# A decoder layer in split fp32: a weight sum made one product earlier, other orders for two kinds of sets, the opening and the closing norm

## The chip, the cores and the metric

The kernel runs on one core of a Trainium2 chip. The metric is the device time of one launch in microseconds. One execution was also profiled; its trace gives the rows that are shown.

## The reference

The layer takes one prompt of 512 tokens, with 16 learned tokens ahead of it, and 8 single sample tokens, in fp32. It layer-normalises the input (2048 wide), projects it to queries, keys, values and a pooling input, runs windowed attention with sinks and a causal pooling mixer, projects both back, and ends with a SwiGLU block between two norms:

```python
h1 = layer_norm(DEEPNORM_ALPHA * h + mix, ln1_g, ln1_b)
a = jax.nn.silu(h1 @ w_gate) * (h1 @ w_up)        # w_gate, w_up: 2048 x 5632
ff = a @ w_down                                   # 5632 x 2048
return layer_norm(DEEPNORM_ALPHA * h1 + ff, ln2_g, ln2_b)
```

(Two lines are shortened here: the reference writes the products as einsum.) What is computed is the same in both kernels.

## The kernel before

**Number format.** TensorE works on operands that are split into a rounded high part and the rest. `split` (L181) makes them from a weight tile: a copy on ScalarE (ACT) for the high half (L185), a subtraction on VectorE (DVE) for the low half (L186). `products` (L198) then issues three matmuls where one would stand: high by high (L201), high by low (L202), low by high (L204).

**Products.** The large matrix products are made in 2 x 2 blocks with seven block products instead of eight (P1 to P7, Winograd's form). For that some operands are sums of weight blocks. `weight_sum` (L191) makes such a sum in place, on DVE (L194), over 128 x 1024 elements. A `Set` (L949) is one tile of 2 x 128 output features of w_gate (g) or w_up (u): four raw weight blocks (r, c), asked for by `q` from the DMA queue of SyncE (SP, L178), and seven products in `run` (L999). `prod` (L966) says which block or sum each takes: P1 takes (0,0), P2 (0,1), P4 (1,1); P7 takes S3 = (0,0) - (1,0), made in the place of (1,0); P6 takes (1,1) - (1,0), again in (1,0); P5 adds (1,0) to (0,0), in (0,0); P3 takes (0,1) - (1,0), in (0,1). Each product is split in two halves (`for g in range(2)`), each of 12 matmuls of 128 x 260.

**Rings.** Raw blocks come from a ring of NRAW = 5 tiles of 512 KB, split halves from a ring of WB = 5. A tile is written again when the tile five places before it in the ring has had its last reader, so the order in which the blocks are asked for decides what a load waits for.

**Sets.** There are 22 pairs (g, u), so 44 sets, and three kinds. In the first pair P1 and P2 are made ahead and stay in PSUM banks (`bk`, NKEEP = 2, "kept"). In the up sets of the next ten pairs P1 is made ahead and copied to SBUF (`p1`, NFILL = 10, "filled"). All others make their P1 themselves. `ahead` (L983) makes these products, before the first set, in plain fp32 (L988). After each product DVE or ACT combines the results: L1010 copies P1, L1022 or L1024 writes c22, L1028 or L1031 c21, L1036 c11, L1041 adds P5's bank to c22, L1045 adds to c21, L1050 writes c12. `al`, `ga`, `de` are PSUM banks; P5 and P3 write `al` after P6, so P3 has to wait until L1041 has read it.

**What sets the order.** On each engine instructions run in the order in which they were placed, one after the other. In most of the kernel a planner places them, by data dependences, its own cost estimates and priorities; loads, splits and weight sums get a priority that lets them go ahead of their place in the code (WPRIO = 400). In the opening the order on TensorE, DVE and ACT is written out by hand: `step` (L158) ties each group of instructions behind the group before.

**Opening (L418 to L480).** For each half h of the tokens the loop over g makes two steps of the key/value projection: `x_norm` (L349, its activation L339) normalises a 512-wide piece of x on ACT (and DVE for the extra rows), `x_turn` (L355, transposes L364) transposes it on TensorE, `x_split` (L366) scales and splits it (L370, L373, L376, L377), `kv_weights` splits weights, `kv_mm` multiplies. `stats` (L304) is a generator for the layer-norm statistics of one row block (L308, L311); those of the second half of x are in `later`, in two parts per block. `normalisers(1)` (L330) makes the factors from them.

**After the sets** the down projection (`column_pair`, L1190) runs in the same form, and the four tile rows that are left (PLAIN) follow as plain blocks: `down(h, m)` (L1295) for two halves of the columns h and 16 row blocks m, 12 matmuls each, added to `acc` by L1308. The closing norm is `Rows` (L1313): `part(q)` transposes a quarter of 128 tokens (L1322) into a bank, takes statistics from it (L1324), copies it to SBUF (L1325); `end` makes mean and deviation and applies them (L1332, L1333), a DMA for each quarter. Tokens of `rows[:2]` are ready after h = 0, those of `rows[2:]` after h = 1.

Of the kernel before, what the change touches and what calls it, by code (L numbers as in the profile page):

```python
# [1 line left out]

# [64 lines left out]
def hybrid_step(ctx, tc, xin, w_in, w_o, w_g, w_u, w_d, w_pool, par_d, cst_d, ident_d, ln2gb, kct_d, vc_d, hist_d,  # L67
                ck_d, cv_d, sp_d, yp, ys, nkp, nvp, npp, nks, nvs, nps):
    nc = tc.nc
# [183 lines left out]
    with ExitStack() as sa:  # L253
# [185 lines left out]
        for h in range(2):  # L439
            for g in range(4):  # L440
                n = h * 4 + g + 1
                with step(*three):
                    x_split(h, 2 * g + 1)
                    if n < 8 and n != 4:
                        x_norm(n // 4, n % 4)
                with step(*three):
                    kv_mm(h, 2 * g)
                if n < 8:
                    with step(*three):
                        x_turn(n // 4, n % 4)  # L450
                        if n < 7:
                            load_kvw((n + 1) % 4)
                        kvw.pop(n % 4, None)
                        kv_weights(n % 4, range(3))
                if h == 0 and g < 2:
                    with step(*three):
                        next(later.pop(0))
                if n < 8:
                    with step(*three):
                        x_split(n // 4, 2 * (n % 4))  # L460
                if n == 2:
                    with step(*three):
                        for x in later:
                            next(x)
                if n == 3:
                    with step(*three):
                        norm[1] = normalisers(1)
                        x_norm(1, 0)
                with step(*three):
                    kv_mm(h, 2 * g + 1)  # L470
                    if n < 8:
                        kv_weights(n % 4, [3])
            with step(*three):
                for i in range(4):
                    if i % 2:
                        nc.vector.tensor_scalar(zkv[i][:, XH[h]], out[i], par[:, PBIAS + i:PBIAS + i + 1], None,
                                                op0=ALU.add)
                    else:
                        nc.scalar.activation(zkv[i][:, XH[h]], out[i], AF.Identity, bias=par[:, PBIAS + i:PBIAS + i + 1])
                if h == 0:  # L480
                    out = kv_banks(1)
# [335 lines left out]
    def bank(name, w=HN):  # L817
        return ps.tile([P, 512], F32, tag="bank", name=name, bufs=banks)[:, :w]
# [130 lines left out]
    class Set:  # L949


        def __init__(self, w, i, name):
            self.w, self.i, self.name = w, i, name
            self.raw, self.bk, self.p1 = {}, {}, None

        def q(self, r, c):
            if (r, c) not in self.raw:
# [4 lines left out]
        def s(self, t, a, b, op):  # L962
            weight_sum(op, self.q(*t), self.q(*a), self.q(*b))
            return self.q(*t)

        def prod(self, n, bk, first=True):  # L966


            b = {1: "b11", 2: "b21", 3: "b22", 4: "t4", 5: "t1", 6: "t2", 7: "t3"}[n]
            src = {1: lambda: self.q(0, 0), 2: lambda: self.q(0, 1), 4: lambda: self.q(1, 1),  # L970
                   7: lambda: self.s((1, 0), (0, 0), (1, 0), nc.vector.tensor_sub),
                   6: lambda: self.s((1, 0), (1, 1), (1, 0), nc.vector.tensor_sub),
                   5: lambda: self.s((0, 0), (1, 0), (0, 0), nc.vector.tensor_add),
                   3: lambda: self.s((0, 1), (0, 1), (1, 0), nc.vector.tensor_sub)}[n]()
            for g in range(2):
                wh, wl = split(src[:, g * 512:(g + 1) * 512], f"{self.name}_{n}{g}")
                for kk in range(4):
                    k = 4 * g + kk
                    sl = slice(kk * P, (kk + 1) * P)
                    hi, lo = bop[b][k // 2]  # L980
                    products([bk], wh[:, sl], wl[:, sl], [hi[:, k % 2, :]], [lo[:, k % 2, :]], k == 0 and first, k == 7, True)
# [17 lines left out]
        def run(self, c11, c12, c21, c22, side=(), out=None):  # L999

            side = iter(side)
            r = row_tile(f"p_{self.name}")
            filled = self.p1 is not None
            al, de = [self.bk.get(n) for n in (1, 2)]
            if not filled:
                self.p1 = r[:, HALF[0]]
                if al is None:
                    al = bank(f"p1_{self.name}")
                    self.prod(1, al)
                nc.scalar.copy(self.p1, al)  # L1010
            else:
                al = bank(f"p1_{self.name}")
            ga = bank(f"p7_{self.name}")
            next(side, None)
            if filled and de is None:

                de = bank(f"p2_{self.name}")
                self.prod(2, de)
            self.prod(7, ga)
            next(side, None)  # L1020
            if filled:
                nc.vector.tensor_add(c22, ga, self.p1)  # L1022
            else:
                nc.scalar.copy(c22, ga)  # L1024
            self.prod(6, al, filled)
            next(side, None)
            if filled:
                nc.vector.tensor_add(c21, al, self.p1)  # L1028
                self.prod(4, ga, False)
            else:  # L1030
                nc.scalar.copy(c21, al)  # L1031
                if de is None:
                    de = bank(f"p2_{self.name}")
                    self.prod(2, de)
            next(side, None)
            nc.vector.tensor_add(c11, de, self.p1)  # L1036
            if out:
                out(0)
            self.prod(5, al, False)
            next(side, None)  # L1040
            nc.vector.tensor_add(c22, c22, al)  # L1041
            if not filled:
                self.prod(4, ga, False)
            next(side, None)
            nc.vector.tensor_add(c21, c21, ga)  # L1045
            if out:
                out(1)
            self.prod(3, al, False)
            if filled:
                nc.vector.tensor_add(c12, al, self.p1)  # L1050
                return c12
            return al
# [61 lines left out]
        bop[n] = [(slot(f"{n}h{i}"), slot(f"{n}l{i}")) for i in range(4)]  # L1114
    turn = [i for i in range(NPAIR) if i not in PLAIN] + [*PLAIN]
    sets = [Set(w, i, f"{n}{i}") for i in turn for n, w in (("g", w_g), ("u", w_u))]
    g1 = ln1(1, zs1)
    fills = [s.ahead(n) for n in (1, 2) for s in sets[:NKEEP]]
    for j, s in enumerate(sets[NKEEP + 1::2][:NFILL]):
# [193 lines left out]
    class Rows:  # L1313
# [4 lines left out]
        def part(self, q):  # L1318
            n, c0 = self.n, self.c0
            tp = bank(f"tz{c0}_{q}", 512)  # L1320
            for i in range(4):
                nc.tensor.transpose(tp[:n, i * P:(i + 1) * P], acc[4 * q + i][:, c0:c0 + n], ident)  # L1322
            z = zp.tile([P, 512], F32, tag="z", name=f"z{c0}_{q}", bufs=NZ)[:n]
            nc.vector.bn_stats(self.st[:n, q, :], tp[:n])  # L1324
            nc.scalar.copy(z, tp[:n])  # L1325
            self.z.append(z)

        def end(self):
            n = self.n
            mu, r = stats_end(pb, self.st, self.mv, n, f"z{self.c0}")  # L1330
            for q, z in enumerate(self.z):
                nc.vector.scalar_tensor_tensor(z, z, mu, gb[0][q][:n], op0=ALU.subtract, op1=ALU.mult)  # L1332
                nc.vector.scalar_tensor_tensor(z, z, r, gb[1][q][:n], op0=ALU.mult, op1=ALU.add)  # L1333
                nc.sync.dma_start(self.dst[:, q * 512:(q + 1) * 512], z)

    def sample_rows():

# [48 lines left out]
    for h, part in ((0, rows[:2]), (1, rows[2:])):  # L1386
        for m in range(KT):
            down(h, m)
            if h == 0 and m in (1, 2):
                for i, q in gb_loads[4 * m - 4:4 * m]:  # L1390
                    nc.sync.dma_start(gb[i][q], ln2gb[i:i + 1, q * 512:(q + 1) * 512].to_broadcast([P, 512]))
            if m % 4 == 3:
                for x in part:
                    x.part(m // 4)
            if (h, m) in ((0, 4), (0, KT - 1), (1, 4), (1, 10), (1, KT - 1)):
                next(sample)
        for x in part:
            x.end()


# [88 lines left out]
```

## Time and profile before

| | us |
|---|---|
| median of 3 runs | 1951.48 (1947.17 to 1955.55) |
| profiled execution | 1948.36 |
| its span, first to last instruction | 1946.5 |
| TensorE busy | 1900.8 (98%) |
| DVE busy | 1542.5 (79%) |
| ACT busy | 935.0 (48%) |
| mean granted TensorE clock | 0.995 |

The stages in the span: opening 0 to 80, attention and pooling to about 340, output projection and the products made ahead to about 590, gate/up sets to about 1450, down projection to about 1850, remainder and closing norm to the end. A row of a timeline gives start, length, engine, line of the kernel, operation, output and input by their names, and in brackets how long the engine was idle before and what ended that. A row that ends in x4 is four instructions in a run. A row of the waits gives engine, its tile and line, what it waited for, then the total, the number of times and the longest one.

### The profile page before, as it was taken

Reading aid. Unit: us, or ns where it says so; the run is one execution under the profiler, and the core shown is the slowest. Engines: PE = TensorE matmul, PEld = TensorE weight load, DVE = VectorE, ACT = ScalarE, POOL = GpSimd, SP = SyncE. Lnnn points to the kernel's source line nnn. Section 1 sums busy time; section 2 is a strip of 40 time slices with the busy share of each in tenths; the row PEclk is TensorE's granted clock in tenths of the full one; section 3 lists DMA queues with packets and bytes.
Section 4 is the critical chain, followed back from the end, with each engine's and each line's share of the span. In section 5 each row is a group of like instructions: output and inputs, shape, how many; then the busy total and the mean of one; then the engine's idle time right before and its main releaser. Section 6 shows DMA issues by size and latency. Waiting matters only on the chain.

```text
span 1946.5 us, 39267 instructions
## 1 busy us (share of the span) xinstructions
PE 1900.8 (98%) x15533; PEld 1865.5 (96%) x15533; DVE 1542.5 (79%) x2734; ACT 935.0 (48%) x1808; POOL 2.7 (0%) x9
## 2 busy tenths in 40 slices
PE   8999999999999999999999999999999999999996
PEld 8999999999989999999999999999999999999996
DVE  6666658768677888888888888888877888888877
ACT  5644445545554444454445555455554443444441
POOL 0000000000000000000000000000000000000000
PEclk9999999999999999999999999999999999999998
DMA  8722222666754444445444534445459564655332
GB/s 268 238 100 71 65 83 81 216 200 196 228 163 143 156 154 157 154 143 173 149 158 146 173 128 152 159 146 171 164 201 370 199 219 164 222 172 202 93 98 89
DMA packets 145240, 319.27 MB, mean 164 GB/s; under 512 B 14288, under 2 KB 66232, under 8 KB 144952
## 3 DMA queue, kind: packets, MB, share of 16 engines
q1 hardware_dynamic: 144480, 315.71, 48.8%
q8 instruction: 122, 2.00, 0.4%
q10 hardware_dynamic: 576, 1.05, 0.2%
q14 instruction: 62, 0.51, 0.1%
HBM read 265.22 MB, written 54.03 MB: 164 GB/s over the span
## 4 chain that ended last, share of the span: by engine, by line
PE 86%; DVE 7%; ACT 3%; DMA 2%; issue 2%; DVEq 0%; ACTq 0%; SPq 0%
PE tri L201 7%; PE tri L204 7%; PE tri L202 6%; PE p_u L201 6%; PE p_u L204 6%; PE p_u L202 6%; PE p_g L204 6%; PE p_g L201 6%; PE p_g L202 6%; PE o L201 3%; PE o L204 3%; PE o L202 3%; DVE rr L186 2%; PE p_u L988 2%; PE mm_u L201 2%
## 5 line engine op out<-in xcount | busy, mean ns | idle before, releaser
L185 ACT CAST rr<-fr 128x512 fp32r<-128x512 f32 (+1 forms) x1056 | 651.6, 643 | 791.4 <-DVE fr L194 298.2
L186 DVE TENSOR_TENSOR rr<-fr,rr 128x512 fp32r<-128x512 f32 (+1 forms) x1056 | 732.5, 717 | 229.9 <-ACT rr L185 219.1
L194 DVE TENSOR_TENSOR fr<-fr 128x1024 f32<-128x1024 f32 (+1 forms) x304 | 320.1, 1053 | 51.8 <-DMA fr<-in_w_g_dram 28.6
L201 PE MATMUL p_g<-rr 128*128 128x260 f32 x830 | 237.1, 286 | 6.1 <-DVE fr L1041 3.2
L204 PE MATMUL p_g<-rr 128*128 128x260 f32 x830 | 232.4, 284 | 4.8 <-DVE rr L186 4.7
L202 PE MATMUL p_g<-rr 128*128 128x260 f32 x788 | 222.5, 283 | 0.0
L201 PE MATMUL p_u<-rr 128*128 128x260 f32 x770 | 217.7, 283 | 1.2 <-DVE fr L1022 1.1
L204 PE MATMUL p_u<-rr 128*128 128x260 f32 x770 | 215.1, 282 | 0.0
L202 PE MATMUL p_u<-rr 128*128 128x260 f32 x748 | 210.8, 282 | 0.0
L204 PE MATMUL tri<-rr 128*128 128x260 f32 x696 | 197.0, 283 | 1.4 <-DVE rr L186 1.4
L201 PE MATMUL tri<-rr 128*128 128x260 f32 x696 | 197.1, 283 | 0.7 <-ACT rr L185 0.7
L202 PE MATMUL tri<-rr 128*128 128x260 f32 x696 | 196.8, 283 | 0.0
L201 PEld LDWEIGHTS p_g<-rr 128*128 128x128 f32 x830 | 156.8, 189 | 10.4 <-ACT fr L1031 5.0
L204 PEld LDWEIGHTS p_g<-rr 128*128 128x128 f32 x830 | 155.8, 189 | 7.3 <-DVE rr L186 7.3
L202 PEld LDWEIGHTS p_g<-rr 128*128 128x128 f32 x788 | 148.8, 189 | 0.0
L201 PEld LDWEIGHTS p_u<-rr 128*128 128x128 f32 x770 | 144.9, 188 | 1.6 <-issue 1.6
L201 PE MATMUL o<-rr 128*128 128x260 f32 x512 | 145.0, 284 | 0.3 <-ACT rr L185 0.3
L204 PEld LDWEIGHTS p_u<-rr 128*128 128x128 f32 x770 | 144.7, 189 | 0.0
L202 PE MATMUL o<-rr 128*128 128x260 f32 x512 | 144.0, 282 | 0.0
L204 PE MATMUL o<-rr 128*128 128x260 f32 x512 | 143.6, 282 | 0.2 <-DVE rr L186 0.2
L202 PEld LDWEIGHTS p_u<-rr 128*128 128x128 f32 x748 | 140.6, 188 | 0.0
L204 PEld LDWEIGHTS tri<-rr 128*128 128x128 f32 x696 | 131.3, 189 | 2.2 <-DVE rr L186 2.0
(319 smaller groups left out, 4562.9 us busy)
## 6 DMA issues: line engine op xcount, KB each, us to landing
fr<-in_w_u_dram SPq DMA_DIRECT2D x100, 512.0 KB
fr<-in_w_g_dram SPq DMA_DIRECT2D x90, 512.0 KB
fr<-in_w_d_dram SPq DMA_DIRECT2D x64, 640.0 KB
t_d<-fr SPq DMA_DIRECT2D x140, 260.0 KB
fr<-in_w_o_dram SPq DMA_DIRECT2D x64, 512.0 KB
fr<-in_w_in_dram SPq DMA_DIRECT2D x48, 512.0 KB
rr<-t_d SPq DMA_DIRECT2D x87, 260.0 KB
mid_b<-t_d SPq DMA_DIRECT2D x53, 260.0 KB
```

Source lines behind the costliest of these rows:

```text
L185: nc.scalar.copy(wh, s)
L186: last_lo[0] = (lo or nc.vector).tensor_sub(wl, s, wh.bitcast(F32)).ins
L194: i = op(*args).ins
L201: nc.tensor.matmul(o, wh, hi[j], start=first, stop=False, skip_group_check=onto)
L202: nc.tensor.matmul(o, wh, lo[j], start=False, stop=False, skip_group_check=onto)
L204: nc.tensor.matmul(o, wl, hi[j], start=False, stop=last, skip_group_check=onto)
L988: nc.tensor.matmul(bk, self.q(0, n - 1)[:, k * P:(k + 1) * P], z1[0][4 * (n - 1) + k // 2][:, k % 2, :], start=(k == 0), stop=(k == 7))
```

## The change

Four things are changed. First, a method `early` makes S3 of a set before `prod(7)` comes to it: in a set that makes its own P1, after the first half-split of that P1; for a set with a kept or filled product, after the first half-split of P3 of the set before it (`next`). Second, filled sets go P7, P2, P6, P4, P5, P3 instead of P2, P7, P6, P4, P5, P3, and kept sets P7, P6, P4, P5, P3 instead of P7, P6, P5, P4, P3. Third, in the opening the statistics of the second half of x, its normalisers and the first `x_norm` of it stand behind the second `kv_mm` of each g and one weight split, instead of before `x_split` and that `kv_mm`; they are spread as one, two and one part over g = 0, 1, 2. Fourth, in the closing norm ACT's copy comes before the statistics, which read the copy in SBUF for the first three quarters, and `end` is a generator: the steps for the first two row blocks are laid between the `down` blocks of h = 1, one after each block and two after every fourth.

```diff
+        def early(self):
+            self.s((1, 0), (0, 0), (1, 0), nc.vector.tensor_sub)
+            self.s3 = True
...
-                   7: lambda: self.s((1, 0), (0, 0), (1, 0), nc.vector.tensor_sub),
+                   7: lambda: self.q(1, 0) if self.s3 else self.s((1, 0), (0, 0), (1, 0), nc.vector.tensor_sub),
...
                 wh, wl = split(src[:, g * 512:(g + 1) * 512], f"{self.name}_{n}{g}")
+                if g == 0 and n == 1:
+                    self.early()
+                if g == 0 and n == 3 and self.next and (self.next.p1 is not None or self.next.bk):
+                    self.next.early()
...
-            if filled and de is None:
+            self.prod(7, ga)
+            next(side, None)
+            kept = de is not None
+            if filled and not kept:
                 de = bank(f"p2_{self.name}")
                 self.prod(2, de)
-            self.prod(7, ga)
-            next(side, None)
...
+            else:
+                nc.scalar.copy(c21, al)
+            if filled or kept:
                 self.prod(4, ga, False)
             else:
-                nc.scalar.copy(c21, al)
-                if de is None:
-                    de = bank(f"p2_{self.name}")
-                    self.prod(2, de)
+                de = bank(f"p2_{self.name}")
+                self.prod(2, de)
...
-            if not filled:
+            if not (filled or kept):
                 self.prod(4, ga, False)
...
-                if h == 0 and g < 2:
-                    with step(*three):
-                        next(later.pop(0))
...
-                if n == 2:
-                    with step(*three):
-                        for x in later:
-                            next(x)
-                if n == 3:
-                    with step(*three):
-                        norm[1] = normalisers(1)
-                        x_norm(1, 0)
                 with step(*three):
                     kv_mm(h, 2 * g + 1)
                     if n < 8:
                         kv_weights(n % 4, [3])
+                if n < 4:
+                    with step(*three):
+                        for _ in range((1, 2, 1)[g]):
+                            next(later.pop(0))
+                        if n == 3:
+                            norm[1] = normalisers(1)
+                            x_norm(1, 0)
...
-            nc.vector.bn_stats(self.st[:n, q, :], tp[:n])
             nc.scalar.copy(z, tp[:n])
+            nc.vector.bn_stats(self.st[:n, q, :], tp[:n] if q == 3 else z)
...
                 nc.vector.scalar_tensor_tensor(z, z, mu, gb[0][q][:n], op0=ALU.subtract, op1=ALU.mult)
+                yield
                 nc.vector.scalar_tensor_tensor(z, z, r, gb[1][q][:n], op0=ALU.mult, op1=ALU.add)
                 nc.sync.dma_start(self.dst[:, q * 512:(q + 1) * 512], z)
+                yield
...
             down(h, m)
+            if h == 1:
+                for _ in range(2 if m % 4 == 1 else 1):
+                    next(ends, None)
...
-        for x in part:
-            x.end()
+        ends = chain.from_iterable([x.end() for x in part])
+    for _ in ends:
+        pass
```

More of the change, by code (lines that the diff above doesn't have):

```diff
@@ L1 @@
 from contextlib import ExitStack, contextmanager
+from itertools import chain
 import concourse.bass as bass
@@ L953, in __init__ @@
             self.w, self.i, self.name = w, i, name
-            self.raw, self.bk, self.p1 = {}, {}, None
+            self.raw, self.bk, self.p1, self.s3, self.next = {}, {}, None, False, None
         def q(self, r, c):
@@ L1116, in hybrid_step @@
     sets = [Set(w, i, f"{n}{i}") for i in turn for n, w in (("g", w_g), ("u", w_u))]
+    for a, b in zip(sets, sets[1:]):
+        a.next = b
     g1 = ln1(1, zs1)
```

## The prediction, made before the change was run

> **What bounds the kernel now.** I read the page's totals and its chain of waits first, then the busy time by stretches, then what TensorE (PE) and VectorE (DVE) waited for, and last the timelines around single stalls.
>
> ```profile
> span 1946.5 us, 39267 instructions
> PE 1900.8 (98%) x15533; PEld 1865.5 (96%) x15533; DVE 1542.5 (79%) x2734; ACT 935.0 (48%) x1808; POOL 2.7 (0%) x9
> ```
> ```profile
> PE 86%; DVE 7%; ACT 3%; DMA 2%; issue 2%; DVEq 0%; ACTq 0%; SPq 0%
> ```
> The kernel is bound by PE, which idles 45.7 us in all (1946.5 - 1900.8). No product is taken away by the change, so it can only win idle time or slow-clock time. Where is that?
>
> ```profile
> 0.00:50.00 50.00, 42.69 (x314) 40.33 (x314) 32.31 (x68) 30.48 (x57) 2.45 (x8) 1.00 0.81 261
> ...
> 600.00:650.00 50.00, 46.75 (x375) 46.36 (x374) 38.64 (x58) 24.09 (x46) 0.00 (x0) 0.97 0.41 143
> ...
> 650.00:1050.00 400.00, 389.88 (x3158) 381.44 (x3157) 339.81 (x545) 193.30 (x366) 0.00 (x0) 1.00 0.46 153
> 1050.00:1400.00 350.00, 350.00 (x2921) 350.00 (x2920) 300.12 (x465) 184.44 (x357) 0.00 (x0) 1.00 0.48 156
> ```
> Columns: stretch, length, then busy time (count) of PE, weight load, DVE, ACT, POOL, then clock, DMA share, GB/s. From 1050 to 1400 (gate/up pairs without a kept product) PE is full: 2921 matmuls in 350 us, 0.120 us each. From 650 to 1050, the ten pairs whose up set has its P1 made beforehand, there are 3158 where that pace would give 400 / 0.120 = 3338. The stretches 0 to 50 and 600 to 650 hold the opening and the first pair, which come further down. The missing 180 are worth 21.6 us, about 2.1 us for each of the ten pairs; the idle share of it is 10.1 us, the rest is matmuls that stand open while their operand comes. This is the largest loss that the change can reach. A pair there takes about 39.3 us (13 products of 24 matmuls, 37.2 us, and 2.1).
>
> ```profile
> PE p_g L204 <- DVE rr L186: 4.7, 10, 0.5
> PE p_g L201 <- DVE fr L1041: 3.2, 1, 3.2
> PE p_g L201 <- ACT fr L1031: 2.9, 10, 0.3
> ```
> ```profile
> DVE fr L194 <- DMA fr<-in_w_g_dram: 23.0, 10, 3.5
> DVE rr L186 <- ACT rr L185: 15.6, 33, 0.7
> DVE fr L194 <- DMA fr<-in_w_u_dram: 13.3, 10, 2.8
> ```
> The first fence is PE over the whole run, the second DVE from 660 to 1040. Ten times each, once a pair, PE waits in the gate set for DVE's low halves (L186), and DVE itself waits once in a gate set (2.3 us on average) and once in an up set (1.3) for a weight sum's (L194) load. DVE is busy 339.81 / 400 x 39.3 = 33.4 us of a pair's 39.3; with 3.6 of load waits and 1.6 for ACT it has nothing left. So here DVE, held by loads, sets PE's pace.
>
> ```profile
> 694.78 1.22 DVE L194 TENSOR_TENSOR fr<-fr 128x1024 f32<-128x1024 f32 x1
> ...
> 696.76 2.50 DVE L186 TENSOR_TENSOR rr<-fr,rr 128x512 fp32r<-128x512 f32 x4 [0.20 <-ACT rr L185]
> ...
> 702.87 1.23 DVE L194 TENSOR_TENSOR fr<-fr 128x1024 f32<-128x1024 f32 x1 [2.54 <-DMA fr<-in_w_g_dram]
> ...
> 717.77 1.29 DVE L186 TENSOR_TENSOR rr<-fr,rr 128x512 fp32r<-128x512 f32 x2
> 718.97 0.42 DVE L1041 TENSOR_TENSOR fr<-fr,p_g 128x260 f32<-128x260 f32 x1
> ...
> 722.22 1.23 DVE L194 TENSOR_TENSOR fr<-fr 128x1024 f32<-128x1024 f32 x1 [1.00 <-DMA fr<-in_w_u_dram]
> ```
> ```profile
> 694.89 3.52 SPq L178 DMA_DIRECT2D fr<-in_w_g_dram  x3
> ...
> 716.34 1.28 SPq L178 DMA_DIRECT2D fr<-in_w_u_dram  x2
> ```
> One such place. u2's last sum (its P3) stands at 694.78, the four low halves after it end at 699.2, and S3 of g3 waits until 702.87. Its (1,0) block was the last of the three loads, issued at 694.89 + 3.52 - 0.33 = 698.08, 4.8 us before; it had to wait for the ring of five raw blocks, whose next one was freed by P3's last low half.
>
> **Part 1 and 2, S3 earlier and P7 first in the up sets.** No arithmetic is added: the same sums (1.22 us), splits and 512 KB loads, in another order. A filled up set now asks for (1,0), (0,0), (0,1), (1,1) instead of (0,1), (1,0), (0,0), (1,1). Counted round the ring of five: the gate set's (1,0) then takes the block that u's own (1,0) held. That is free after P3's sum (694.78 + 1.22 = 696.0), not after its last low half (698.08). Its load comes 2.0 us earlier, so S3 of the gate set could start at 700.8 in place of 702.87, and the 2.54 us wait shrinks by 2.0.
>
> What is late next is the up set. Its (0,0) takes the place of g's (0,0), free after g's P5 low halves; that is the load at 716.34. With the same 4.8 us it lands at 721.2, so S3 of u3 starts at 721.2 instead of 722.22. But up to now DVE filled part of this wait with the low halves of u's P2; with P7 first, S3 stands ahead of them. After L1041 (718.97 + 0.42 = 719.4) DVE then idles 1.8 us in place of the 1.00, so 0.8 comes back. Per pair 0.8 - 2.0 = -1.2 us, times 10 = **-12 us**. The bounds: -2.1 a pair where DVE has other work for the wait (PE is full then, as from 1050 on), and for the worse end the rows of the first pair (below). I take -1.2, since DVE with 33.4 of 37.2 us has little to fill in. Of SP's queue: the (0,1) load is moved behind two loads, and the stores between them (L1105) stay; P2's block is needed only after P7, 2.9 us later.
>
> In sets without a kept product S3 moves before the second half of their own P1's split. From 1050 to 1400 PE has no wait; DVE is busy 300.12 of 350. The work that hides a shift there is P1 itself (2.9 us), and if that cover went, each of 11 pairs could lose up to S3's 1.2 us: 0 taken, 0 to +13.
>
> The first pair (g0, u0, both P1 and P2 kept) begins with P7 already, and its S3 stands ahead of L1041 already:
>
> ```profile
> 603.42 1.22 DVE L194 TENSOR_TENSOR fr<-fr 128x1024 f32<-128x1024 f32 x1 [1.58 <-DMA fr<-in_w_u_dram]
> 604.56 0.42 DVE L1041 TENSOR_TENSOR fr<-fr,p_g 128x260 f32<-128x260 f32 x1
> ```
> ```profile
> 605.13 0.36 PE L201 MATMUL p_g<-rr 128*128 128x260 f32 x1 [3.17 <-DVE fr L1041]
> ```
> ```profile
> 606.40:609.78 3.38, 3.38 (x18) 3.38 (x17) 1.52 (x2) 0.13 (x2) 0.00 (x0) 0.50 0.02 5
> 609.78:613.20 3.42, 3.42 (x30) 3.42 (x29) 2.43 (x3) 1.89 (x5) 0.00 (x0) 1.00 0.00 0
> ```
> PE waits 3.17 us because c22 += al (L1041), which frees the bank that P3 writes, is behind the waiting S3 in DVE's queue. Then the clock is at 0.50 for 3.38 us, half of that lost: 1.7. The change leaves this order, so I take 0; the bound is -4.9.
>
> The Trainium skill, "TensorE: Matmul & The Clock Gate", Part 1 (The HAM clock gate), says that TensorE's clock is halved after about one idle window of 3.4 us and is full again after a busy window as long, the windows running free of the kernel. This row agrees: 3.17 us idle, then 3.38 us at half clock. By that rule stalls under 2 us cost only themselves.
>
> **Part 3, opening.** DVE and ACT run in the written order.
>
> ```profile
> 26.52 1.28 DVE L308 BATCH_NORM_STATS2 mid_a<-fr 128x6 f32<-128x512 f32 x2
> ...
> 37.87 2.47 DVE L308 BATCH_NORM_STATS2 mid_a<-fr 128x6 f32<-128x512 f32 x4
> ```
> ```profile
> 48.49 1.52 ACT L339 ACTIVATE fr<-fr,mid_a 128x512 f32<-128x512 f32 x2 [1.22 <-DVE mid_a L334]
> 49.91 0.60 ACT L185 CAST rr<-fr 128x512 fp32r<-128x512 f32 x1
> ```
> ```profile
> 29.05 0.92 PE L201 MATMUL kv<-rr 128*128 128x276 f32 x4 [0.96 <-ACT rr L376]
> ...
> 41.23 0.40 PE L204 MATMUL kv<-rr 128*128 128x276 f32 x1 [0.93 <-DVE rr L186]
> ...
> 50.57 0.40 PE L201 MATMUL kv<-rr 128*128 128x276 f32 x1 [1.40 <-ACT rr L185]
> ```
> The statistics of x's second half stand ahead of what PE wants next, and each time PE waits: 0.96 + 0.93 + 1.40 = 3.3 us. Behind kv_weights they no longer do. What is late next: normalising the second half (1.52 on ACT, after DVE's normalisers) now comes about 1 us later before x_turn(1, 0), and each moved pair of statistics (1.28) stands ahead of the next x_split. I give back 1.3 for one such wait of PE: **-2.0 us**, bounds -3.3 and +1.
>
> **Part 4, closing norm.**
>
> ```profile
> 1915.42 5.39 DVE L1333 SCALAR_TENSOR_TENSOR mid_c<-mid_c,fr 128x512 f32<-128x512 f32 x8
> 1920.72 1.29 DVE L1324 BATCH_NORM_STATS2 fr<-tz 128x6 f32<-128x512 f32 x2
> ...
> 1929.60 1.30 DVE L1324 BATCH_NORM_STATS2 fr<-tz 128x6 f32<-128x512 f32 x2 [0.45 <-PE tz L1322]
> ```
> ```profile
> 1922.09 0.38 PE L201 MATMUL d<-rr 128*128 128x256 f32 x1 [1.88 <-ACT mid_c L1325]
> ```
> ```profile
> 1930.33 1.18 ACT L1325 COPY mid_c<-tz 128x512 f32<-128x512 f32 x2 [1.01 <-DVE fr L1324]
> ```
> The lump of eight multiplications (L1333, 0.67 us each) holds the statistics, these hold ACT's copy, and that holds a bank: 1.88 us of PE. Laid between 16 blocks of `down` (12 matmuls, 1.4 us each), one 0.67 us step with one 0.42 us addition fits, and the copy now goes first: -1.88. At the end the last statistics wait for a copy (0.6): +0.6. What follows PE's end (two rows' norm, 13 us of DVE) stays. **-1.3 us**; bounds -2.2 and +1. The moved stores on SP have nothing behind them that PE needs.
>
> **Sum.** -12 - 2.0 - 1.3 = -15.3. The profiled execution took 1948.4 us (span 1946.5 and 1.9 around it): 1933.1. The median of the runs, 1951.5, is 3.1 above it: **1936 us**.
>
> **Rivals.**
>
> A, the stalls vanish whole: filled pairs run at the pace of 1050 to 1400, -21, with -3.3 from the ends about **1927**. For it: DVE has 33.4 us of work in 37.2. Against: the up set's (0,0) still hangs on g's P5, and S3 has lost P2's cover.
>
> B, the stall only moves: the early S3 stands in DVE's queue ahead of L1041 in every gate set, as at 603.42. S3 would end at 721.2 + 1.2 = 722.4, L1041 at 722.8, so P3 starts at about 723.0:
>
> ```profile
> 715.62 0.39 PE L201 MATMUL p_g<-rr 128*128 128x260 f32 x1 [0.29 <-ACT fr L1031]
> ...
> 721.48 0.28 PE L201 MATMUL p_g<-rr 128*128 128x260 f32 x1
> ```
> P5 starts at 715.62 and P3 at 721.48, with half of P4 between them. PE would wait 1.5 to 1.9 there in place of the 2.1 removed: pairs unchanged, **1948**. That the change doesn't do what it says, because a load decides where S3 runs anyway, gives the same time.
>
> C, slower: as B, but with all of P4 put ahead of P5, as it is in the first pair. Then nothing covers the wait for L1041 and each pair pays what that pair shows, 3.17 + 1.7 = 4.9 in place of 2.1: +2.8 x 10 - 3.3 = +25, about **1976**. It decides once L1041 comes over 3 us after P5's end with no half product left between. For it: it is the only place in the trace where a set begins with P7. Against: PE now has half of P4 between P5 and P3. By the page named above the slow clock belongs to such stalls; without it C is 1959.
>
> **Chances.** Forecast 0.40, A 0.17, B 0.25, C 0.18. A measurement of this kernel tells about 0.5%, 9.8 us, from no change. The forecast's own range is 1929 to 1943 (pairs at -1.9 to -0.5), four fifths of it beyond that limit: faster 0.32 + 0.17 = 0.49; same 0.08 + 0.25 = 0.33; slower 0.18. The range holds A, the forecast, B and the mild end of C: 1923 to 1960.
>
> **What would show it.** Right: DVE's waits for w_g loads fall from 23.0 to some 3, those for w_u rise from 13.3 to some 20; L204's ten waits of 0.5 and L1031's of 0.3 go; 650 to 1050 holds about 3260 matmuls; PE's waits at 29.05, 41.23, 50.57 and 1922.09 are gone. B or C: PE p_g L201 waits for DVE L1041 ten times, in C with the clock at 0.50 behind it. I am wrong if PE's wait in the gate set stays while S3 comes earlier (then loads are not what holds DVE), or if the stretch after 1050 loses its full PE.

## The result, and the profile after

The change makes the kernel slower: 1969.16 us (median of 4 runs, 1964.52 to 1971.2) against 1951.43 us, a ratio of 1.0088 (95% interval 1.0059 to 1.0116), so 0.9%. The forecast was 1936, its range 1923 to 1960. The profiled execution took 1964.52 us, 16.2 more than the one of before (1948.36).

In the changed file helper lines stand one line further down (L186 is ACT's high half, L187 DVE's low half, L195 the weight sum, L202, L203 and L205 the three matmuls), and L1049 is the addition that was L1041. The page's totals and the busy time by stretches of the kernel after:

```profile
span 1962.7 us, 39311 instructions
PE 1898.8 (97%) x15533; PEld 1864.6 (95%) x15533; DVE 1538.6 (78%) x2734; ACT 943.9 (48%) x1808; POOL 2.7 (0%) x9
```
```profile
0.00:50.00 50.00, 44.91 (x330) 42.05 (x331) 33.47 (x70) 31.62 (x59) 2.46 (x8) 1.00 0.83 271
50.00:100.00 50.00, 49.21 (x400) 47.91 (x401) 35.67 (x68) 30.30 (x61) 0.00 (x0) 1.00 0.75 247
...
600.00:650.00 50.00, 45.87 (x378) 45.24 (x377) 38.63 (x59) 23.40 (x45) 0.00 (x0) 1.00 0.41 136
650.00:1050.00 400.00, 368.49 (x3005) 362.29 (x3005) 323.51 (x525) 188.09 (x349) 0.00 (x0) 1.00 0.46 146
1050.00:1400.00 350.00, 350.00 (x2922) 350.00 (x2921) 297.36 (x459) 188.45 (x355) 0.00 (x0) 1.00 0.47 154
```

PE does the same work with 18.2 us more idle time. The loss is in one place: 650 to 1050 holds 3005 matmuls in place of 3158, 153 x 0.12 = 18.4 us. 0 to 50 gained 16 matmuls (314 to 330), and 1050 to 1400 is as full as before. PE's waits over the whole run, then DVE's from 660 to 1040:

```profile
PE p_g L205 <- DVE rr L187: 16.2, 10, 2.0
PE p_u L202 <- ACT rr L186: 9.4, 10, 1.6
PE p_g L202 <- ACT rr L186: 7.1, 11, 0.6
...
PE p_g L202 <- DVE fr L1049: 3.0, 1, 3.0
```
```profile
DVE fr L195 <- DMA fr<-in_w_u_dram: 36.3, 9, 4.6
DVE fr L195 <- DMA fr<-in_w_g_dram: 29.5, 10, 3.1
```

The gate sets' wait for low halves grew from 4.7 to 16.2 us, and it now stands at another place, in P1. A new wait of ten times 0.9 us came at the up sets, a third of up to 0.6 us at eleven half products of the gate sets (7.1 us), and DVE's waits for loads went from 36.3 (23.0 + 13.3) to 65.8. They were to fall for w_g. Where do the first two PE waits come from? DVE's timeline of g3 and u3, then PE's, then SP's queue:

```profile
701.66 1.22 DVE L195 TENSOR_TENSOR fr<-fr 128x1024 f32<-128x1024 f32 x1 [3.12 <-DMA fr<-in_w_g_dram]
702.80 0.68 DVE L187 TENSOR_TENSOR rr<-fr,rr 128x512 fp32r<-128x512 f32 x1
...
717.55 1.90 DVE L187 TENSOR_TENSOR rr<-fr,rr 128x512 fp32r<-128x512 f32 x3
...
720.65 0.42 DVE L1049 TENSOR_TENSOR fr<-fr,p_g 128x260 f32<-128x260 f32 x1
725.33 1.23 DVE L195 TENSOR_TENSOR fr<-fr 128x1024 f32<-128x1024 f32 x1 [4.26 <-DMA fr<-in_w_u_dram]
```
```profile
703.54 0.39 PE L205 MATMUL p_g<-rr 128*128 128x260 f32 x1 [1.73 <-DVE rr L187]
```
```profile
727.32 0.39 PE L202 MATMUL p_u<-mid_b,rr 128*128 128x260 f32 x1 [1.21 <-ACT rr L186]
```
```profile
719.23 1.30 SPq L179 DMA_DIRECT2D fr<-in_w_u_dram  x2
```

First place: S3 of g3 (701.66) stands in DVE's queue ahead of the low half of the second half of g3's own P1 (702.80). DVE idles 3.12 us for S3's load, and PE, in the middle of P1, waits for that low half until 703.54. Second place: S3 of u3 waits 4.26 us for the (0,0) block, whose load was issued at 719.23 and landed 6.1 us later. PE is through with g3 (its P3 ended about 726) and now begins u3 with P7, which needs S3; P2, which needs no sum, stands behind it. The third wait (7.1 us) is no part of the loss: it is as long in e12_ask_no_own and e14_order_ask below, which lose next to nothing in the pairs.

### The profile page after: what moved, and what is told of

It reads as the page before. It is cut to its first block, busy times and chain, and to the rows that moved or that the text cites. A ratio compares the mean times of both kernels' runs of the same rounds, so it can differ in the third digit from the quotient of the medians.

```text
span 1962.7 us, 39311 instructions
## 1 busy us (share of the span) xinstructions
PE 1898.8 (97%) x15533; PEld 1864.6 (95%) x15533; DVE 1538.6 (78%) x2734; ACT 943.9 (48%) x1808; POOL 2.7 (0%) x9
## 4 chain that ended last, share of the span: by engine, by line
PE 75%; DVE 11%; DMA 7%; issue 4%; ACT 2%; SPq 0%; DVEq 0%; ACTq 0%
PE tri L202 6%; PE tri L205 6%; PE tri L203 6%; DVE rr L187 5%; PE p_u L202 5%; PE p_u L203 5%; PE p_u L205 5%; PE p_g L205 5%; PE p_g L202 4%; PE p_g L203 4%; DMA fr<-in_w_g_dram 3%; DMA fr<-in_w_u_dram 3%; PE o L202 3%; PE o L205 3%; PE o L203 3%
## 5 line engine op out<-in xcount | busy, mean ns | idle before, releaser
L186 ACT CAST rr<-fr 128x512 fp32r<-128x512 f32 (+1 forms) x1056 | 658.2, 643 | 798.5 <-DVE fr L195 276.1
L187 DVE TENSOR_TENSOR rr<-fr,rr 128x512 fp32r<-128x512 f32 (+1 forms) x1056 | 737.4, 717 | 214.4 <-ACT rr L186 203.1
L195 DVE TENSOR_TENSOR fr<-fr 128x1024 f32<-128x1024 f32 (+1 forms) x304 | 319.9, 1052 | 82.6 <-DMA fr<-in_w_u_dram 46.2
L205 PE MATMUL p_g<-rr 128*128 128x260 f32 x830 | 231.5, 283 | 16.2 <-DVE rr L187 16.2
L202 PE MATMUL p_g<-rr 128*128 128x260 f32 x830 | 235.6, 285 | 10.0 <-ACT rr L186 7.1
L203 PE MATMUL p_g<-rr 128*128 128x260 f32 x788 | 221.7, 282 | 0.0
L202 PE MATMUL p_u<-rr 128*128 128x260 f32 x770 | 217.6, 283 | 0.0
L205 PE MATMUL p_u<-rr 128*128 128x260 f32 x770 | 215.3, 282 | 0.0
L203 PE MATMUL p_u<-rr 128*128 128x260 f32 x748 | 210.7, 282 | 0.0
L205 PE MATMUL tri<-rr 128*128 128x260 f32 x696 | 196.9, 283 | 1.1 <-DVE rr L187 1.1
L202 PE MATMUL tri<-rr 128*128 128x260 f32 x696 | 197.1, 283 | 0.8 <-ACT rr L186 0.8
L203 PE MATMUL tri<-rr 128*128 128x260 f32 x696 | 196.8, 283 | 0.0
L205 PEld LDWEIGHTS p_g<-rr 128*128 128x128 f32 x830 | 155.1, 189 | 18.2 <-DVE rr L187 18.2
L202 PEld LDWEIGHTS p_g<-rr 128*128 128x128 f32 x830 | 156.2, 188 | 12.5 <-ACT rr L186 9.4
L203 PEld LDWEIGHTS p_g<-rr 128*128 128x128 f32 x788 | 148.1, 188 | 0.0
L202 PE MATMUL o<-rr 128*128 128x260 f32 x512 | 145.0, 284 | 0.3 <-ACT rr L186 0.3
L202 PEld LDWEIGHTS p_u<-rr 128*128 128x128 f32 x770 | 144.9, 188 | 0.2 <-ACT rr L186 0.2
L205 PEld LDWEIGHTS p_u<-rr 128*128 128x128 f32 x770 | 144.7, 189 | 0.0
L203 PE MATMUL o<-rr 128*128 128x260 f32 x512 | 144.0, 282 | 0.0
L205 PE MATMUL o<-rr 128*128 128x260 f32 x512 | 143.6, 282 | 0.2 <-DVE rr L187 0.2
L203 PEld LDWEIGHTS p_u<-rr 128*128 128x128 f32 x748 | 140.6, 188 | 0.0
L205 PEld LDWEIGHTS tri<-rr 128*128 128x128 f32 x696 | 131.3, 189 | 1.8 <-DVE rr L187 1.6
```

What stands on the lines that cost most here:

```text
L186: nc.scalar.copy(wh, s)
L187: last_lo[0] = (lo or nc.vector).tensor_sub(wl, s, wh.bitcast(F32)).ins
L195: i = op(*args).ins
L202: nc.tensor.matmul(o, wh, hi[j], start=first, stop=False, skip_group_check=onto)
L203: nc.tensor.matmul(o, wh, lo[j], start=False, stop=False, skip_group_check=onto)
L205: nc.tensor.matmul(o, wl, hi[j], start=False, stop=last, skip_group_check=onto)
```

## The experiments

All comparisons are with the kernel before on the same chip. As a common measure of the ten filled pairs I use the matmuls between 650 and 1050 us; each one fewer than 3158 is 0.12 us. (It is good to some 2 us: a run with the set code of before, below, shows 3140.) Medians in the text come from several chips, so runs are compared by their ratios and matmuls. The last two columns are waits for loads from 660 to 1040 us: those of DVE, and those of ACT's splits (L186), which read raw blocks for P1, P2 and P4. T1 to T7 are the theories of the texts on record.

| run | orders | early S3: own P1 / P3 before | ratio (interval) | matmuls | DVE's load waits, w_g + w_u | ACT's, w_u |
|---|---|---|---|---|---|---|
| before | P2 first | - / - | 1 | 3158 | 23.0 + 13.3 | 0 |
| after | P7 first | yes / yes | 1.0088 (1.0059 to 1.0116) | 3005 | 29.5 + 36.3 | 0 |
| e6_ends | P2 first | - / - | 0.9975 (0.9965 to 0.9985) | 3140 | 23.3 + 14.5 | 0 |
| e1_no_own | P7 first | - / yes | 1.0045 (1.0028 to 1.0062) | 3045 | 16.2 + 41.7 | 0 |
| e3_own_late | P7 first | late / yes | 1.0041 (1.0026 to 1.0056) | 3076 | 15.9 + 39.7 | 0 |
| e2_no_next | P7 first | yes / - | 1.0073 (1.0058 to 1.0088) | 2997 | 30.1 + 36.2 | 0 |
| e9_order_only | P7 first | - / - | 1.0028 (1.0015 to 1.0041) | 3029 | 15.6 + 43.6 | 0 |
| e5_loads_only | P7 first | loads only | 1.0038 (1.0025 to 1.0051) | 3074 | 15.2 + 40.3 | 0 |
| e4_p2_first | P2 first | yes / yes | 1.0011 (1.0001 to 1.0020) | 3139 | 11.9 + 23.1 | 9.2 |
| e8_p2_no_next | P2 first | yes / - | 0.9982 (0.9970 to 0.9993) | 3143 | 25.4 + 14.2 | 0 |
| e10_store_pool | P7 first | yes / yes | 1.0073 (1.0058 to 1.0087) | 3012 | 24.2 + 37.2 | 0 |
| e11_ask_order | P7 first, new asking | yes / yes | 1.0044 (1.0029 to 1.0059) | 3046 | 23.3 + 0.9 | 17.4 |
| e12_ask_no_own | P7 first, new asking | - / yes | 0.9996 (0.9984 to 1.0007) | 3144 | 17.4 + 0.4 | 23.4 |
| e14_order_ask | P7 first, new asking | - / - | 0.9989 (0.9978 to 1.0000) | 3153 | 16.0 + 0.4 | 23.9 |

**The parts alone.** Four runs: without S3 in a set's own P1, with it after both half-splits, with P2 first again, and only the ends.

```diff
 e1_no_own
-                if g == 0 and n == 1:
-                    self.early()
 e3_own_late
-                if g == 0 and n == 1:
+                if g == 1 and n == 1:
                     self.early()
 e4_p2_first
-            self.prod(7, ga)
-            next(side, None)
             kept = de is not None
             if filled and not kept:
                 de = bank(f"p2_{self.name}")
                 self.prod(2, de)
+            self.prod(7, ga)
+            next(side, None)
 e6_ends: class Set of the kernel before, opening and closing norm of the changed one
```

> The changed kernel without S3 ahead in a set's own P1; the next kept or filled set's S3 is still made in P3. Theory T1 (S3, put ahead of the second low half of its own P1, waits there for its load and holds that half: 2.0 us in each of ten gate sets): PE's ten waits p_g L205 <- DVE go from 16.2 us to at most the 4.7 of the kernel before, time 1949 to 1956; the up set's ten waits for ACT (9.4 us) stay. Rival T2 (the loads come late by their order in the ring, wherever the sum is put): PE waits as long at g's P7 instead, 1965 to 1970.

> The changed kernel with S3 of a set's own P1 placed after both half-splits of P1, so its two blocks are still asked for early but the sum stands behind both low halves. T1: the wait of 2.0 us goes, 1946 to 1954, a little under the run without it. T2: as the changed kernel, 1965 to 1970.

> The changed kernel with P2 ahead of P7 again in the filled sets. T1: the gate set's wait of 2.0 us stays, the up set's wait of 1.6 us at P7 is covered by P2: 1951 to 1957. T2: PE's waits keep their sum, 1965 to 1970.

> The sets of the kernel before, with the opening and the closing norm of the changed one. By the changed kernel's own trace the opening is worth -2.0 and the closing -0.8: 1948 to 1950 where the kernel before takes 1951.4, if all the loss is in the sets; if the 1.5 us lost again by the end of the output projection come from the opening, 1950 to 1951. Rival: the ends take part in the loss, 1953 or more.

e1_no_own took 1961.8 us, between the two expectations. The waits p_g L205 went as T1 said, but it gave back only 40 matmuls (4.8 us): the up sets' wait for ACT grew to 16.0 us.

```profile
PE p_u L202 <- ACT rr L186: 16.0, 11, 2.4
```

e3_own_late took 1959.9, again between the two expectations, and is like it (14.1 us at that place). So the wait behind the own P1 is real, but taken away alone it mostly hands its time to the next one. e4_p2_first took 1954.9, in T1's range, and brings back 134 of the 153 matmuls. T1's reason does not hold there, though: it said that the gate sets' wait would stay, and that fell from 16.2 to 0.9 us. e6_ends took 1947.9: the opening and the closing are no part of the loss.

**Which of the orders and early sums.** 

```diff
 e9_order_only: both calls of early() taken out
 e8_p2_no_next: e4_p2_first without self.next.early()
 e2_no_next: the changed kernel without self.next.early()
 e5_loads_only
         def early(self):
-            self.s((1, 0), (0, 0), (1, 0), nc.vector.tensor_sub)
-            self.s3 = True
+            self.q(1, 0), self.q(0, 0)
```

> The changed kernel without any early S3: only the orders of the sets, the opening and the closing norm are changed. The run with P2 first took 15 us off the ten filled pairs' loss of 20. Theory T3 (P7 ahead of P2 in the filled up sets is the loss: P2's two halves were the work that ran while the load for S3 was on its way): PE waits for ACT's high half at the up sets' P7, ten pairs 10 to 25 us over the kernel before, time 1958 to 1975. Rival T4 (P7 first costs only because an early S3 blocks DVE): pairs within 3 us of the kernel before, 1947 to 1953.

> P2 first in the filled sets, S3 early only in a set's own P1, not in the P3 of the set before. T3: pairs within 3 us of the kernel before, 1949 to 1956. T4: the S3 in the set's own P1 still holds its second low half, ten pairs 8 us or more over the kernel before, 1957 or more.

> The changed kernel without S3 in the P3 of the set before (P7 first, S3 early in the set's own P1). T3: the loss stays, 1962 to 1976, since the up set's S3 then comes no earlier. T4: half of the loss goes, 1955 to 1962.

> The changed kernel with the two blocks asked for where S3 was made early, but S3 itself made at P7 as before. T3: the loss at the up set's P7 stays, 1958 to 1972. T4: both waits shrink, 1948 to 1956.

The order alone (e9_order_only, 1960.2) loses 129 matmuls, 15.5 us, with no early S3 in it; the up sets' wait at P7 is 17.7 us.

```profile
PE p_u L202 <- ACT rr L186: 17.7, 10, 2.5
```

With P2 first the edit for the own P1 costs nothing that shows (e8_p2_no_next, 1951.7, 3143). That does not test an S3 that stands in the way: the planner put S3 behind both low halves of g3's P1 there, as in the kernel before (four low halves from 696.98, S3 at 702.07). With P7 first, keeping only that one (e2_no_next, 1970.3) is as slow as the change, and asking early without summing early (e5_loads_only, 1960.2) is like having no early S3. T3 stands, and T4 falls by e9_order_only: P7 ahead of P2 in the filled up sets, with the blocks asked for in that order, is the main loss. The profiled execution of e9_order_only took 1969.2, 9 above its median, so its 15.5 is rather an upper value; the ratio says 1.0028, where the same ends without the order have 0.9975: 0.5%, 10 us.

**Why: late block, or order as such?** Two edits on the changed kernel, and two on e6_ends that move the asking alone.

```diff
 e11_ask_order (next.early(True) at the call)
-        def early(self):
+        def early(self, nxt=False):
+            if nxt and self.p1 is not None:
+                self.q(1, 0), self.q(0, 1)
 e10_store_pool: in staged(), the loop over go[1], t12, t34
-                nc.sync.dma_start(t_d[i, n:n + 2, :, j, :]...
+                nc.gpsimd.dma_start(t_d[i, n:n + 2, :, j, :]...
 b1_ask, in run()
+            for x in ((0, 1), (1, 0), (1, 1), (0, 0)) if filled else ((0, 0), (0, 1), (1, 1), (1, 0)):
+                self.q(*x)
 b2_ask_g, in run()
+            if not filled and not self.bk:
+                for x in ((0, 0), (0, 1), (1, 1), (1, 0)):
+                    self.q(*x)
```

> The changed kernel, P7 first as it stands, but a filled up set asks for its blocks in the order (1,0), (0,1), (0,0), (1,1) in place of (1,0), (0,0), (0,1), (1,1): (0,0), which S3 needs, then takes the block of g's (1,0), free after g's P3 sum (715.76 in the changed kernel's trace), not that of g's (0,0), whose load was issued at 719.23. T3 (the loss is the wait for this load with P2's cover gone): it comes 3.4 us earlier, PE's ten waits for ACT at the up sets' P7 (9.4 us) go, 1950 to 1961. Rival T5 (the order of the products costs by itself, through DVE's and ACT's queues, whenever the load lands): 1965 to 1971.

> The changed kernel with the stores of the staged activations issued from POOL instead of SP. In the changed kernel's trace the (0,0) load stands behind such a store on SP (718.78, then the load at 719.23, where its block is free at 718.24). If the queue is part of it: 1.0 us earlier in each of ten pairs, 1958 to 1964. If it is only the block's release: 1966 to 1971.

> The sets of the kernel before with the changed opening and closing norm, and the blocks asked for at the start of a set: gate sets (0,0), (0,1), (1,1), (1,0), filled up sets (0,1), (1,0), (1,1), (0,0). No product and no sum is moved. The gate set's (1,0) then takes the block that u's (1,1) leaves (lo of P4, 691.3 in the trace of before) instead of 698.08; u's (0,0) takes g's (1,1) (717.25 instead of 715.13). If S3's load is what costs the filled pairs 2.1 us: DVE's waits for w_g (23.3) fall under 8, pairs -10 to -20, 1928 to 1940. If DVE's own work sets the pace: pairs within 4 us, 1944 to 1951.

> As the run before it, but only the gate sets ask in the new order; the filled up sets ask as in the kernel before, (0,1), (1,0), (0,0), (1,1). The gate set's (1,0) takes u's (0,0) block (lo of P5, 694.9 instead of 698.08), u's (0,0) takes g's (0,1) or (1,1), 717 to 719 instead of 715.13. If S3's load costs the pairs their 2.1 us: 1930 to 1943, a little behind the run before it. If not: 1944 to 1953.

e11_ask_order: (0,0) comes from a block that is free earlier, DVE's waits for w_u fall from 36.3 to 0.9 and PE's ten waits at the up sets' P7 are gone (9.4 to 1.1). So that wait was the late block. ACT's splits of the raw block for P2 now wait for loads instead, 17.4 us. And the time is 1962.0, a little over T3's range, since the gate sets' wait stays:

```profile
PE p_g L205 <- DVE rr L187: 17.1, 10, 2.3
```

e10_store_pool (1967.2, 3012): with the stores off SP's queue nothing is won, and S3 of u3 still waits 5.05 us for its load. The store that stands ahead of the load on SP is not the cause of that wait. (The gate sets' wait falls to 2.3 us in this run, but a wait for L1049 of 9.7 us comes at the up sets.)

b1_ask (1967.8, ratio 1.0076, 1.0064 to 1.0088; 3074 matmuls) and b2_ask_g (1993.5, 1.0205, 1.0188 to 1.0221; 2839) missed both expectations. In b1_ask DVE's waits for w_g are gone altogether, as meant. But ACT's splits wait 16.7 us for w_g where they had no such wait, and the up sets pay too:

```profile
728.47 1.23 DVE L195 TENSOR_TENSOR fr<-fr 128x1024 f32<-128x1024 f32 x1 [4.38 <-DMA fr<-in_w_u_dram]
```
```profile
719.64 1.32 SPq L179 DMA_DIRECT2D fr<-in_w_u_dram  x2
```

Two blocks of u3 were asked for in the 1.32 us from 719.64, the second at 720.23 by the trace, and a third at 721.60. S3 could start at 728.47, 8.2 us after the second. DVE's waits for w_u come to 33.8 us. In b2_ask_g they come to 39.6. The sets after 1050, which ask in the new order too, lose as well: 2877 and 2848 matmuls for 2921. In both runs what one set or engine wins by another order of asking, another loses.

**Both PE waits away.**

```diff
 e12_ask_no_own: e11_ask_order without early() in the own P1
 e14_order_ask: e9_order_only with, in run(),
+            if filled:
+                self.q(1, 0), self.q(0, 1)
```

> As the run with the new asking order for filled up sets, (1,0), (0,1), (0,0), (1,1), P7 first, but without S3 early in a set's own P1. T3 with T1 (the loss is two waits: the up set's S3 for its late block, and the gate set's early S3 ahead of its P1's second low half): both are gone, PE's waits p_g L205 fall from 17.1 to under 3, pairs 15 to 20 us under the 447.4 of that run, 1941 to 1947, faster than the kernel before. T5 (the order of products costs by itself): pairs stay over 440, 1955 or more.

> The same asking order and orders of products, with no early S3 at all. If S3 made early is worth nothing by itself: within 2 us of the run before it. If S3 in the P3 of the set before is worth something: 4 us or more slower in the pairs.

e12_ask_no_own took 1951.9 and e14_order_ask 1950.6, with 3144 and 3153 matmuls: the 18 us are back, to within 2 by this count. By the ratio they stay 4 and 3 us behind e6_ends (0.9996 and 0.9989 for 0.9975), the second within the intervals. From the changed kernel's 3005, taking away the own early S3 gives +40, the new asking order +41, both together +139. So the loss is these two waits, and each alone is worth little: with one gone, PE stands at the other. e12_ask_no_own did not get under the kernel before, where 1941 to 1947 were expected, and e14_order_ask shows that S3 made early is worth nothing there by itself. DVE's waits for loads in e14_order_ask, and ACT's:

```profile
DVE fr L195 <- DMA fr<-in_w_g_dram: 16.0, 10, 2.3
DVE fr L195 <- DMA fr<-in_w_u_dram: 0.4, 2, 0.2
```
```profile
ACT rr L186 <- DMA fr<-in_w_u_dram: 23.9, 9, 3.2
```

On DVE 16.4 us are left of 36.3, and PE is no faster (3153 against 3158). But the waits have moved, not gone: (0,1), the raw block of P2, now comes late, and ACT waits for it, where the kernel before has no such wait. Both engines together wait 40.3 us. No run on record has a smaller total than the 36.3 of the kernel before, so none shows what PE would do with fewer load waits. In the table, but for e11_ask_order, the matmuls go with the total: 36 to 44 us have 3139 to 3158, 55 to 66 us have 2997 to 3076. That speaks for the loads and does not prove it, since e11_ask_order has 41.6 and 3046, b2_ask_g 45.5 and 2839.

**What the 2.1 us are.** One guess for PE's waits that are left is that ACT takes splits out of the code's order. Two runs tie ACT's splits in the sets to that order, on e6_ends and on e14_order_ask.

```diff
-            nc.scalar.copy(wh, s)
+            hi = nc.scalar.copy(wh, s).ins
+            if seq:
+                if last_hi[0] is not None:
+                    tc.add_manual_dep(hi, last_hi[0].name, mybir.DependencyInfo(mybir.DependencyClass.NoSync,
+                                                                                mybir.DependencyReason.DATA), reason="seq")
+                last_hi[0] = hi
```

> The sets of the kernel before with the changed opening and closing norm (the run of that kind took 1947.9), and ACT's splits in the sets tied to the order of the code. T6 (the 2.1 us a pair come from splits taken out of order, which hold places of the ring of five): PE's waits p_g L202 <- ACT and p_g L205 <- DVE in the gate sets go, ten pairs 5 to 20 us shorter, 1928 to 1943. T7 (DVE's and ACT's work, or S3's load, sets the pace): within 4 us, 1944 to 1952.

> The same tie on the run with P7 first, the new asking order and no early S3 (1950.6). T6: 5 to 20 us shorter, 1931 to 1945; and with S3's loads earlier here than in the run beside it, not behind it by more than 2 us. T7: 1946 to 1955.

T6 falls: 1959.2 (ratio 1.0023, 1.0012 to 1.0035; 3074 matmuls) and 1975.4 (1.0114, 1.0094 to 1.0134; 2950), both slower than without the tie and outside T7's ranges too. The planner's own order of splits is better than the code's. What the 2.1 us a pair are made of stays open: the order of the splits is not it, in this form, and no run settles whether the loads are.

## Why the prediction was wrong, point by point

**What holds PE in the filled pairs** was not tested. The prediction read DVE as full (33.4 us of work and 3.6 of load waits in 39.3) and took a shorter load wait of DVE for PE time won. The change made these waits longer, and in e14_order_ask, where DVE loses 20 us of them, ACT has 23.9 us of new ones. So this step stays open. The sign that the prediction set against itself did come: S3 of the gate sets came a little earlier, and PE's wait there did not go but grew to 16.2 us, in P1, behind the waiting S3.

**The 2.0 us at the gate set** were mis-sized. The load did move up as counted round the ring: S3 starts 7.4 us after the sum of P3 before it (694.26 to 701.66), not 8.1 (694.78 to 702.87).

```profile
694.37 1.46 SPq L179 DMA_DIRECT2D fr<-in_w_g_dram  x2
```

It was issued at 695.50 (694.37 + 1.46 - 0.33) and landed 6.1 us later, not 4.8, so 0.7 came of the 2.0.

**"0.8 comes back" at the up set** is the step of the forecast that failed most. The block was the right one (free after g's P5 low halves, here at about 718.2 in place of 716.3), but its load was issued at 719.23 and took 6.1 us, so DVE idled 4.26 us where 1.8 were worked out. Of the 2.5 us more, 1.3 are the load. The kernel before showed as much at this place: S3 of u3 started 5.9 us after the load at 716.34 (722.22), so the gate set's 4.8 should not have been used here. And the price was taken in DVE's idle time alone. What P2 first had covered was PE: its 2.9 us of product ran while S3 was on its way. The text named that cover under rival A and did not price it; e9_order_only and e4_p2_first put it at 10 to 16 us over ten pairs, and e11_ask_order shows that the late (0,0) block is behind PE's wait.

**S3 in the own P1** was put at "0 taken, 0 to +13", for the sets after 1050 only, where it holds (2922 matmuls in 350 us). The gate sets of the ten filled pairs have an own P1 too, and there the load is late: ten waits, 16.2 us. This was left out of the sum. These two steps are the loss: with both waits gone, in e12_ask_no_own, the 18 us are back.

**Rival C** had the sign and something like the size (+25), not the mechanism, so its nearness is luck: PE waits for L1049 once, 3.0 us, in the first pair, not in each. **Rival B's** waits at P3 did not come either. Both took S3 to stand ahead of that addition in DVE's queue; in the changed kernel L1049 (720.65) comes before S3 (725.33).

**The first pair** was taken as unchanged, bound -4.9. The stall stayed (3.17 to 3.0), but this time the clock stayed at 1.00 (600 to 650: 0.97 before, 1.00 after). By the row of before that is 1.7 us won, by luck (see the last section).

**The opening** was right in its mechanism and got half its size, -1.1 for -2.0. By 100 us there are 17 matmuls more (713 to 730), 2.0 us, but 0.92 us of that was there at the first `kv` matmul, before any instruction that was moved, and 1.97 at the last one:

```profile
20.08 0.39 PE L201 MATMUL kv<-rr 128*128 128x276 f32 x1 [1.33 <-ACT rr L185]
```
```profile
19.16 0.39 PE L202 MATMUL kv<-rr 128*128 128x276 f32 x1 [1.33 <-ACT rr L186]
```

(The first of before.) That the 2.0 was met is luck. The waits at 29.05, 41.23 and 50.57 are gone, and the one that the text gave back came where it said, at x_turn, with 1.26 us for the 1.3. By these rows it would be 2.0 us again; what took the rest is not shown.

```profile
48.44 0.30 PE L365 MATMUL xt<-fr,mid_a 128*128 128x128 f32 x1 [1.26 <-DVE fr L371]
```

**The closing norm** was nearly right. The wait of 1.88 is gone. The first `d` matmul came 16.97 us later than before, the last multiplications 16.14:

```profile
1886.88 0.28 PE L202 MATMUL d<-rr 128*128 128x264 f32 x1
```
```profile
1953.62 5.38 DVE L1345 SCALAR_TENSOR_TENSOR mid_c<-mid_c,fr 128x512 f32<-128x512 f32 x8
```
```profile
1869.91 0.28 PE L201 MATMUL d<-rr 128*128 128x264 f32 x1
```
```profile
1937.48 5.39 DVE L1333 SCALAR_TENSOR_TENSOR mid_c<-mid_c,fr 128x512 f32<-128x512 f32 x8
```

(The first two of the kernel after, the others of before.) That is -0.8 for -1.3. The tail behind PE costs more than the 0.6 worked out: ACT's copies of the third quarter come late too, at 1943.4 after 2.03 us of waiting for PE's transposes, so four statistics instead of two stand behind PE's last block. The lump of eight is still there in the planned order, five and three around one addition of `down` (from 1932.60); that the copy goes ahead of it is enough. The ends together are worth 0.25% (e6_ends, 0.15 to 0.35%), which is 4.9 us and more than the 2.8 us of the two rows. The 2 us between are within what executions of one kernel differ by.

**Two slips in the working** change nothing: 13 products of 24 matmuls at 0.12 us are 37.4 us, not 37.2, and of the range 1929 to 1943 nine tenths, not four fifths, lie beyond the limit of 9.8 us.

## What to carry to other kernels

An engine's wait for a load is no gain to be had until the engine that sets the end is shown to wait for it: look for that engine's own waits. When a wait for loads has gone from one engine, look for it on all the others that read loaded blocks before calling it gone. Before a product that needs a late operand is moved ahead of one that needs none, price the cover on the engine that computes, not on the one that prepares. A sum that is moved up in an in-order queue holds everything behind it until its last operand lands, and with a ring of five blocks an earlier request for one block is a later one for another.

## What was not expected of the hardware

A stall of about 3 us brings the half clock in one run and not in another. At the same place, 3.17 us of PE idle gave 3.38 us at 0.50 in the kernel before, and 2.51 us gave 3.4 us at 0.50 in e3_own_late (603.80 to 607.20); 3.0 us in the kernel after and 3.11 in e11_ask_order gave none. So the length of the stall alone does not decide, and the idle window of 3.4 us that the prediction went by is no safe limit. The Trainium skill, "TensorE: Matmul & The Clock Gate", Part 1 (The HAM clock gate), calls the window free-running. These rows fit that; that it is the place of the stall in the window that decides is not shown by any run here. The clock also fell in a stretch in which PE shows no idle time:

```profile
296.80:300.20 3.40, 3.40 (x26) 3.40 (x26) 3.33 (x17) 3.29 (x14) 0.00 (x0) 0.82 0.50 155
300.20:303.60 3.40, 3.40 (x21) 3.40 (x21) 2.53 (x10) 2.32 (x11) 0.00 (x0) 0.68 0.49 153
```

It was 0.82 and 0.68 in the kernel after (1.00 in both stretches before), which is 1.7 us lost, as much as the kernel before lost at the first pair. What brought it is not shown.

A load's time is not a constant of its size. From its issue to the sum that waited for it, a 512 KB load on the same queue took 4.8 and 5.9 us in the two places of the kernel before, 6.1 in both places after, and 8.2 in b1_ask, where three loads and three stores were issued within 4 us. By the issues and landings that the traces keep, such loads between 660 and 1040 us took 3.5 to 8.1 us in the kernel before (median 5.0) and 3.6 to 8.4 after (median 5.9). That it is what is issued with a load that makes it longer fits the rows and is not shown by a run of its own.
